# The MLP's last 512 output columns as 384 and 128, with a bank of their own for the 128

## The chip, the cores and the metric

The kernel runs on one core of one Trainium2 chip. The metric is the device time of one execution in microseconds. Of the kernel before three runs were timed; their median is the number to compare with.

## The reference

Two transformer blocks run one after the other on x (256 tokens, width 1024, float32). The change touches only the end of the second block: the squared-ReLU MLP, its residual, and the final norm.

```python
def squared_relu_mlp(h, w_up, w_down):
    a = jax.nn.relu(h @ w_up)
    return (a * a) @ w_down
...
        x = x + squared_relu_mlp(rms_norm(x, g_mlp), w_up, w_down)
    return rms_norm(x, g_final)
```

w_up is 1024 by 4096 and w_down 4096 by 1024. The norm of h multiplies a whole token row by one number r; since relu(a)² scales with r², the kernel leaves r out of the matmuls and multiplies the MLP's output by r² at the end.

## The kernel before

Every product of float32 matrices is made from two parts: `split` turns a piece of weights into a high part `wh` (ACT, rounded to the matmul's format) and a low part `wl` (DVE, the rest), and three matmuls stand for one: high by high, high by low, low by high.

The MLP (`mlp`) works in eight stages of 512 hidden columns. `up` makes a stage's hidden activations `t` (a high and a low tile), `down` multiplies the previous stage's with 512 rows of w_down and adds into four PSUM banks that live through the whole MLP: `acc[c][tt]` for column half c (512 columns) and token tile tt (128 tokens). These banks have the tag "mm"; the hidden activations' sums use the four banks of tag "at".

The last stage is `down_last` (lines 1334 to 1359). It loads both column halves, splits them into four pairs (`parts`), and then runs, for token tile 0 and then 1, and for column half 0 and then 1, a piece of twelve matmuls of 512 columns into `acc[c][tt]`. Behind each piece stand: the update of x on DVE (line 1350, a `scalar_tensor_tensor` that multiplies the bank by r² and adds x), the sum of squares of the 512 columns (`square_sum`, line 651), and the product with the final gain on DVE (line 1352). When both halves of a token tile are done, DVE adds the two sums and epsilon (line 1354), POOL takes the reciprocal root (line 1355), each half is scaled by it (`scaled`, line 646), and SP stores it (line 1359): two stores of 256 KB for each token tile.

The order of instructions on each engine is not the order of writing. All operations are first recorded (`Plan.record`), then `Plan.order` (line 162) runs them through a list of estimated costs (`cost`, line 131) and latencies (line 126): whenever an engine is free, it takes the ready operation with the lowest rank. The rank (line 262) is the index at recording, plus a bias, plus a shift by engine and kind of the output tile:

```python
        prio = [o["i"] + o["bias"] + SHIFT.get((o["engine"], o["kind"]), 0) for o in self.ops]
...
SHIFT = {("tensor", "mm"): 100, ("vector", "wl"): -20}
```

The kind is the tile's tag (line 54). An operation recorded by `either` (line 115) has two forms, one on ACT and one on DVE, and takes the engine that is free first; `square_sum` and `scaled` are such. Matmuls into one bank keep their order. A tag has a fixed number of buffers (4 for `wh`, 4 for `wl`), and a tile's turn comes when an earlier one's last reader is done, so that the four pairs of the last stage are split one by one as the stage before frees them. The resulting order is fixed when the program is built; on the chip each engine goes through its list in order and waits on semaphores.

All instructions carry line 284, the helper that issues them, in the profile, so they are told apart by tile names: `t_mm` and `t_at` are the PSUM banks, `t_p` the scratch that the square sum writes, `t_xg` the product with the gain, `t_rstd` the small tiles of the root.

Of the kernel before, what the change touches and what calls it, by code (L numbers as in the profile page):

```python
# [12 lines left out]
AF = mybir.ActivationFunctionType  # L13
ALU = mybir.AluOpType
AX = mybir.AxisListType

P = 128
# [3 lines left out]
EPS = 1e-6  # L21
# [286 lines left out]
class Kernel:  # L308
# [341 lines left out]

    def square_sum(self, v, ms):

        junk = self.work("p", [P, 512], PB)
        self.nc.either(("scalar", "activation", (junk, v, AF.Square), {"scale": 1.0 / 32.0, "accum_out": ms}),
                       ("vector", "tensor_tensor_reduce", (),
                        {"out": junk, "in0": v, "in1": v, "scale": 1.0 / D, "scalar": 0.0, "op0": ALU.mult,
                         "op1": ALU.add, "accum_out": ms}))
# [635 lines left out]
    def mlp(self, ms):  # L1293
        nc, a = self.nc, self.a
        hT = self.turns("n", [self.x[:, :, :512], self.x[:, :, 512:]], "mlp")
        self.flush("n")
        r = self.rstd(ms)
        r2 = self.work("rstd", [P, 2], 4)
        nc.vector.tensor_tensor(r2, r, r, ALU.mult)
        NS = 8  # L1300
        gb = self.slot([P, D], "gb", F32)
        nc.gpsimd.dma_start(gb, a["g_final_2"].rearrange("(o d) -> o d", o=1).to_broadcast([P, D]))
        xg = [self.slot([P, 2, 512], "xg", F32) for _ in range(2)]

        def square(t, f, n, po):
            r = self.work("tanh", [P, 2, S], 2)[:, :n]
            nc.scalar.activation(r, po, AF.Relu)
            q = self.work("p", [P, 2, S], PB)[:, :n]
            nc.scalar.activation(q, r, AF.Square)
            self.hilo(t[0][:, f:f + n, :], t[1][:, f:f + n, :], q)  # L1310

        def up(s):
            t = self.y_tiles()
            for i in range(2):
                square(t, 2 * i, 2, self.proj_t(a["w_up_2"], 512 * s + 256 * i, hT, tag="at"))
            return t

        def up_first():
            t = self.y_tiles()
            po = [self.psum("at" if f < 2 else "mm")[:, 0] for f in range(4)]  # L1320
            for c in range(2):
                raw = self.load(a["w_up_2"], c * 512, 4, 0, 512)
                for i in range(2):
                    wh, wl = self.split(raw[:, :, 256 * i:256 * i + 256])
                    for f in range(2):
                        fs = slice(f * P, (f + 1) * P)
                        for k in range(4):
                            self.mm3(po[2 * i + f], wh[:, k, fs], wl[:, k, fs], hT(0, 4 * c + k), hT(1, 4 * c + k),
                                     c == 0 and k == 0, c == 1 and k == 3)
            for f in range(4):  # L1330
                square(t, f, 1, po[f].unsqueeze(1))
            return t

        def down_last(s, t):
            parts = [list(self.wide(a["w_down_2"], 512 * s, 4, 512 * c)) for c in range(2)]
            parts = [[(k0, *self.split(v)) for k0, v in half] for half in parts]
            for tt in range(2):
                ts = slice(tt * P, (tt + 1) * P)
                ms = self.work("ms", [P, 2, 2], 4)
                for c in range(2):  # L1340
                    o = acc[c][tt]
                    for k0, wh, wl in parts[c]:
                        for j in range(2):
                            xh, xl = t[0][:, k0 + j, ts], t[1][:, k0 + j, ts]
                            self.nc.tensor.matmul(o, xh, wh[:, j, :], start=False, stop=False)
                            self.nc.tensor.matmul(o, xh, wl[:, j, :], start=False, stop=False)
                            self.nc.tensor.matmul(o, xl, wh[:, j, :], start=False, stop=k0 + j == 3)
                    cs = slice(512 * c, 512 * c + 512)
                    xv = self.x[:, tt, cs]
                    nc.vector.scalar_tensor_tensor(xv, o, r2[:, tt:tt + 1], xv, ALU.mult, ALU.add)  # L1350
                    self.square_sum(xv, ms[:, c, 0:1])
                    nc.vector.tensor_tensor(xg[c][:, tt, :], xv, gb[:, cs], ALU.mult)
                r = self.work("rstd", [P, 2], 4)[:, :1]
                nc.vector.scalar_tensor_tensor(r, ms[:, 0, 0:1], EPS, ms[:, 1, 0:1], ALU.add, ALU.add)
                nc.gpsimd.tensor_tensor(r, r, self.mhalf[:, :1], ALU.pow)
                for c in range(2):
                    v = xg[c][:, tt, :]
                    self.scaled(v, v, r)
                    nc.sync.dma_start(self.out[0, tt * P:(tt + 1) * P, 512 * c:512 * c + 512], v)

        def down(s, t):
            for c in range(2):
                self.proj_n(self.wide(a["w_down_2"], 512 * s, 4, 512 * c), 4, 512, lambda l, k: t[l][:, k, :],
                            banks=acc[c], start=s == 0, stop=False)

        t = up_first()
        acc = [[self.psum("mm", [P, 512]) for _ in range(2)] for _ in range(2)]
        for s in range(NS - 1):
            t2 = up(s + 1)
            down(s, t)  # L1370
            t = t2
        down_last(NS - 1, t)

    def run(self, upto=99):
# [34 lines left out]
PB = 4  # L1409
# [81 lines left out]
```

## Time and profile before

| what | value |
|---|---|
| timed runs | 779.42, 780.11, 781.40 us |
| median | 780.11 us |
| profiled execution | 779.68 us |
| its span, first to last instruction | 777.9 us |
| mean granted clock of TensorE | 0.995 |
| instructions | 11758 |

The profile is of one execution. A line of the timeline has the start, the duration, the engine, the output and input tiles, the shape, and in brackets how long the engine was idle before and what released it. DVE is VectorE, ACT ScalarE, POOL GpSimd, SP SyncE, PE TensorE and PEld its weight loads. The ends of matmuls are modelled, so steps between matmuls are read from start to start. A stretch of busy times gives for each engine the busy time and in brackets the number of instructions.

### The profile page before, as it was taken

What the parts mean: (1) busy time and instruction counts of PE and PEld (TensorE: products, weight loads), DVE (VectorE), ACT (ScalarE), POOL (GpSimd) and SP (SyncE); (2) the same over time, 40 slices, a digit from 0 to 9 for tenths busy, and PEclk for the clock granted to TensorE, in tenths of its full rate; (3) what the DMA queues carried; (4) which work ended last, traced back from release to release, by engine and by line L of the source; (5) the groups of instructions that cost most, each with busy time, mean ns of one, the idle gap of its engine ahead of it and who ended that gap; (6) DMA issues with size and microseconds to landing.
All of it is one profiled execution on the core that took longest, in us unless ns stands there. A gap on an engine that the chain in (4) does not pass through costs nothing.

```text
span 777.9 us, 11758 instructions
## 1 busy us (share of the span) xinstructions
PE 763.1 (98%) x4320; PEld 661.2 (85%) x4320; DVE 620.0 (80%) x1127; ACT 536.8 (69%) x1046; POOL 74.7 (10%) x105
## 2 busy tenths in 40 slices
PE   8989999999999999999999999999999999999996
PEld 7678898888888888888888898799989888888885
DVE  5999998998779889979988889976677655565554
ACT  6697987876679669757787787465556765556552
POOL 0640010000001421132011100100000000000000
PEclk9999999999999999999999999999999999999998
DMA  7796546445558855765348645356535565655631
GB/s 231 244 285 216 162 127 227 138 137 176 184 186 260 237 159 157 210 202 190 115 156 242 191 120 193 105 179 217 181 118 164 177 185 180 215 191 187 210 115 54
DMA packets 109989, 140.48 MB, mean 181 GB/s; under 512 B 3779, under 2 KB 81539, under 8 KB 109932
## 3 DMA queue, kind: packets, MB, share of 16 engines
q1 hardware_dynamic: 104460, 131.64, 52.5%
q0 software_dynamic: 5472, 8.10, 4.7%
q8 instruction: 34, 0.56, 0.3%
q14 instruction: 23, 0.19, 0.1%
HBM read 134.98 MB, written 1.06 MB: 175 GB/s over the span
## 4 chain that ended last, share of the span: by engine, by line
PE 86%; DVE 5%; issue 3%; POOL 2%; ACT 2%; DMA 1%; SPq 0%; POOLq 0%; DVEq 0%; ACTq 0%
PE t_mm L284 64%; PE t_at L284 22%; DVE t_wl L284 2%; DVE t_y L284 1%; POOL t_rrs L284 1%; POOL t_rstd L284 1%; DMA t_xT<-in_x_t_dram 1%; POOL t_ks L284 1%; ACT t_wh L284 0%; DVE t_xs L284 0%; DVE t_p L284 0%; DVE t_x L284 0%; ACT t_p L284 0%; ACT t_xg L284 0%; ACT t_mT L284 0%
## 5 line engine op out<-in xcount | busy, mean ns | idle before, releaser
L284 DVE TENSOR_TENSOR t_wl<-t_raw,t_wh 128x1024 fp32r<-128x1024 f32 (+1 forms) x237 | 288.8, 1219 | 72.6 <-ACT t_wh L284 70.9
L284 ACT ACTIVATE t_wh<-t_raw 128x1024 fp32r<-128x1024 f32 (+1 forms) x237 | 250.4, 1058 | 74.2 <-PE t_mm L284 61.3
L284 PE MATMUL t_mm<-t_mT,t_wh 128*128 128x512 f32 (+1 forms) x512 | 181.6, 394 | 0.4 <-ACT t_wh L284 0.4
L284 PE MATMUL t_mm<-t_mT,t_wl 128*128 128x256 f32 x496 | 131.9, 284 | 0.0
L284 PE MATMUL t_mm<-t_wh,t_yh 128*128 128x512 f32 x288 | 113.5, 394 | 0.0
L284 PE MATMUL t_mm<-t_wh,t_yl 128*128 128x512 f32 x288 | 112.9, 393 | 0.0
L284 PE MATMUL t_mm<-t_wl,t_yh 128*128 128x512 f32 x288 | 112.7, 391 | 0.0
L284 PEld LDWEIGHTS t_mm<-t_mT,t_wh 128*128 128x128 f32 x512 | 93.7, 188 | 14.0 <-ACT t_wh L284 0.8
L284 PEld LDWEIGHTS t_mm<-t_mT,t_wl 128*128 128x128 f32 x496 | 93.4, 189 | 6.5 <-DVE t_wl L284 0.3
L284 PE MATMUL t_at<-t_mT,t_wh 128*128 128x512 f32 (+1 forms) x256 | 85.7, 382 | 0.0
L284 ACT COPY t_sum<-t_mm 128x256 f32<-128x256 f32 x97 | 36.0, 371 | 55.6 <-PE t_mm L284 55.1
L284 PE MATMUL t_mm<-t_wh,t_gh 128*128 128x256 f32 (+2 forms) x256 | 65.9, 339 | 1.5 <-ACT t_wh L284 1.5
L284 PE MATMUL t_at<-t_mT,t_wl 128*128 128x256 f32 x240 | 63.8, 280 | 0.0
L284 PEld LDWEIGHTS t_mm<-t_wh,t_yl 128*128 128x128 f32 x288 | 54.1, 188 | 11.1
L284 PEld LDWEIGHTS t_mm<-t_wl,t_yh 128*128 128x128 f32 x288 | 54.1, 188 | 10.8
L284 PEld LDWEIGHTS t_mm<-t_wh,t_yh 128*128 128x128 f32 x288 | 54.1, 188 | 10.5 <-ACT t_yh L284 0.2
L284 PE MATMUL t_mm<-t_hT,t_wh 128*128 128x512 f32 x168 | 61.8, 400 | 1.0 <-DVE t_sum L284 1.0
L284 ACT ACTIVATE t_p<-t_p,t_st 128x256 f32<-128x256 f32 (+1 forms) x111 | 52.6, 493 | 9.6 <-DVE t_st L284 9.4
L284 POOL TENSOR_TENSOR t_rstd<-t_rstd,t_mhalf 128x2 f32<-128x2 f32 (+1 forms) x12 | 13.3, 1107 | 457.3 <-DVE t_rstd L284 457.3
L284 PEld LDWEIGHTS t_at<-t_mT,t_wh 128*128 128x128 f32 x256 | 45.8, 188 | 6.8
L284 DVE TENSOR_TENSOR t_sum<-t_mm,t_sum 128x256 f32<-128x256 f32 x97 | 40.8, 421 | 13.5 <-ACT t_sum L284 12.7
L284 PEld LDWEIGHTS t_mm<-t_wh,t_gh 128*128 128x128 f32 x256 | 45.1, 194 | 5.9 <-ACT t_wh L284 1.7
(177 smaller groups left out, 1389.1 us busy)
## 6 DMA issues: line engine op xcount, KB each, us to landing
t_raw<-in_w_in_odd_dram SPq DMA_DIRECT2D x20, 1024.0 KB, 5.2
t_raw<-in_w_up_dram SPq DMA_DIRECT2D x16, 1024.0 KB, 5.7
t_raw<-in_w_down_dram SPq DMA_DIRECT2D x16, 1024.0 KB, 5.0
t_raw<-in_w_in_dram SPq DMA_DIRECT2D x12, 1024.0 KB, 5.5
t_raw<-in_w_in_even_dram SPq DMA_DIRECT2D x10, 1024.0 KB, 5.1
t_raw<-in_w_mem_kv_dram SPq DMA_DIRECT2D x8, 1024.0 KB, 5.2
t_raw<-in_w_out_even_dram SPq DMA_DIRECT2D x6, 1024.0 KB, 5.6
t_raw<-in_w_out_odd_dram SPq DMA_DIRECT2D x6, 1024.0 KB, 5.3
```

The costliest lines, as they stand in the source:

```text
L284: f(*[self.real(v) for v in args], **{k: self.real(v) for k, v in kwargs.items()})
```

## The change

In the last stage, token tile 1's second column half is computed as two pieces: columns 0 to 383 into the bank as before, and columns 384 to 511, for this last stage alone, into a bank of their own with the tag "at". The bank `acc[1][1]` keeps the sums of the first seven stages for these 128 columns. After the 384-column piece DVE updates all 512 columns of x from the old bank; a second update then adds the new bank to the last 128. The sum of squares is taken over 384 and over 128 columns apart, a further DVE addition joins the third sum, and the products with the gain for these two cuts are recorded behind the root (`held`). Token tile 0 and all first halves keep pieces of 512.

For both token tiles the scaling is no longer left to `scaled`: DVE scales the first half and the last 128 columns of the second, ACT the other 384. SP stores the first half, and ACT issues the store of the second.

`square_sum` takes as much of its scratch as its input has columns.

```diff
-        junk = self.work("p", [P, 512], PB)
+        junk = self.work("p", [P, 512], PB)[:, :v.shape[-1]]
...
-                ms = self.work("ms", [P, 2, 2], 4)
-                for c in range(2):
-                    o = acc[c][tt]
+                ms = self.work("ms", [P, 2, 2], 4).rearrange("p a b -> p (a b)")
+                held = []
+                cuts = [(0, 0, 512), (1, 0, 512)] if tt == 0 else [(0, 0, 512), (1, 0, 384), (1, 384, 512)]
+                for i, (c, b0, b1) in enumerate(cuts):
+                    bs = slice(b0, b1)
+                    own = b0 > 0
+                    o = self.psum("at", [P, 512])[:, bs] if own else acc[c][tt][:, bs]
                     for k0, wh, wl in parts[c]:
                         for j in range(2):
                             xh, xl = t[0][:, k0 + j, ts], t[1][:, k0 + j, ts]
-                            self.nc.tensor.matmul(o, xh, wh[:, j, :], start=False, stop=False)
-                            self.nc.tensor.matmul(o, xh, wl[:, j, :], start=False, stop=False)
-                            self.nc.tensor.matmul(o, xl, wh[:, j, :], start=False, stop=k0 + j == 3)
-                    cs = slice(512 * c, 512 * c + 512)
+                            self.nc.tensor.matmul(o, xh, wh[:, j, bs], start=own and k0 + j == 0, stop=False)
+                            self.nc.tensor.matmul(o, xh, wl[:, j, bs], start=False, stop=False)
+                            self.nc.tensor.matmul(o, xl, wh[:, j, bs], start=False, stop=k0 + j == 3)
+                    full = slice(512 * c, 512 * c + 512)
+                    cs = slice(512 * c + b0, 512 * c + b1)
+                    if not own:
+                        nc.vector.scalar_tensor_tensor(self.x[:, tt, full], acc[c][tt], r2[:, tt:tt + 1],
+                                                       self.x[:, tt, full], ALU.mult, ALU.add)
                     xv = self.x[:, tt, cs]
-                    nc.vector.scalar_tensor_tensor(xv, o, r2[:, tt:tt + 1], xv, ALU.mult, ALU.add)
-                    self.square_sum(xv, ms[:, c, 0:1])
-                    nc.vector.tensor_tensor(xg[c][:, tt, :], xv, gb[:, cs], ALU.mult)
+                    if own:
+                        nc.vector.scalar_tensor_tensor(xv, o, r2[:, tt:tt + 1], xv, ALU.mult, ALU.add)
+                    self.square_sum(xv, ms[:, i:i + 1])
+                    held.append((xg[c][:, tt, bs], xv, gb[:, cs]))
+                    if b1 - b0 == 512:
+                        nc.vector.tensor_tensor(*held.pop(), ALU.mult)
                 r = self.work("rstd", [P, 2], 4)[:, :1]
-                nc.vector.scalar_tensor_tensor(r, ms[:, 0, 0:1], EPS, ms[:, 1, 0:1], ALU.add, ALU.add)
+                nc.vector.scalar_tensor_tensor(r, ms[:, 0:1], EPS, ms[:, 1:2], ALU.add, ALU.add)
+                if tt == 1:
+                    nc.vector.tensor_tensor(r, r, ms[:, 2:3], ALU.add)
                 nc.gpsimd.tensor_tensor(r, r, self.mhalf[:, :1], ALU.pow)
-                for c in range(2):
-                    v = xg[c][:, tt, :]
-                    self.scaled(v, v, r)
-                    nc.sync.dma_start(self.out[0, tt * P:(tt + 1) * P, 512 * c:512 * c + 512], v)
+                for v in held:
+                    nc.vector.tensor_tensor(*v, ALU.mult)
+                rows = slice(tt * P, (tt + 1) * P)
+                v = [xg[c][:, tt, :] for c in range(2)]
+                nc.vector.tensor_scalar(v[0], v[0], r, None, ALU.mult)
+                nc.sync.dma_start(self.out[0, rows, :512], v[0])
+                nc.scalar.activation(v[1][:, :384], v[1][:, :384], AF.Copy, scale=r)
+                nc.vector.tensor_scalar(v[1][:, 384:], v[1][:, 384:], r, None, ALU.mult)
+                nc.scalar.dma_start(self.out[0, rows, 512:], v[1])
```

## The prediction

> **What bounds the kernel now.** I read the page first (engine shares, chain), then the busy times by stretch over the end of the run, then the timeline there, because the diff edits only the last stage of the MLP.
>
> ```profile
> span 777.9 us, 11758 instructions
> PE 763.1 (98%) x4320; PEld 661.2 (85%) x4320; DVE 620.0 (80%) x1127; ACT 536.8 (69%) x1046; POOL 74.7 (10%) x105
> PE 86%; DVE 5%; issue 3%; POOL 2%; ACT 2%; DMA 1%; SPq 0%; POOLq 0%; DVEq 0%; ACTq 0%
> ```
>
> TensorE is busy for 98% of the span and holds 86% of the chain of waits: a matmul added before its last one lengthens the run, and otherwise only the tail behind the last matmul counts. The next view gives the stretches of the end, columns named in its first line.
>
> ```profile
> core 0: us, PE busy (x) PEld busy (x) DVE busy (x) ACT busy (x) POOL busy (x), PEclk, DMA share, GB/s
> 759.96:762.68 2.72, 2.72 (x14) 2.25 (x13) 1.23 (x1) 1.06 (x1) 0.00 (x0) 1.00 0.00 0
> ...
> 768.12:770.84 2.72, 2.72 (x13) 1.91 (x11) 1.59 (x3) 1.21 (x3) 0.00 (x0) 1.00 0.51 193
> 770.84:773.28 2.44, 0.00 (x1) 0.00 (x0) 1.60 (x3) 0.72 (x2) 0.56 (x1) 1.00 0.00 0
> ...
> 774.63:776.13 1.50, 0.00 (x0) 0.00 (x0) 0.00 (x0) 0.00 (x0) 0.00 (x0) 0.50 0.93 350
> 776.13:777.90 1.77, 0.00 (x0) 0.00 (x0) 0.00 (x0) 0.00 (x0) 0.00 (x0) 0.50 0.00 0
> ```
>
> Each piece of twelve 512-column matmuls (one token tile, one column half) takes 2.72 us on a TensorE without gaps, so 0.227 us a matmul; four such pieces are the last, 759.96 to 770.84. Then comes a tail of 7.06 us: 2.44 to the reciprocal root, the scaling, 1.5 us in which the last 512 KB run at a 0.93 busy DMA, and 1.77 of completion and closing. The timeline of the tail:
>
> ```profile
> 770.45 0.39 PE L284 MATMUL t_mm<-t_wh,t_yl 128*128 128x512 f32 x1
> 770.88 0.75 DVE L284 SCALAR_TENSOR_TENSOR t_x<-t_mm,t_rstd,t_x 128x512 f32<-128x512 f32 x1 [1.13 <-PE t_mm L284]
> 771.66 0.69 DVE L284 TENSOR_TENSOR t_xg<-t_x,t_gb 128x512 f32<-128x512 f32 x1
> 771.72 0.63 ACT L284 ACTIVATE t_p<-t_x 128x512 f32<-128x512 f32 x1 [1.94 <-DVE t_x L284]
> 772.26 0.19 ACT L284 ACTIVATION_READ_ACCUMULATOR t_p<-t_x 128x1 f32 x1
> 772.48 0.16 DVE L284 SCALAR_TENSOR_TENSOR t_rstd<-t_ms 128x1 f32<-128x1 f32 x1
> 772.72 0.56 POOL L284 TENSOR_TENSOR t_rstd<-t_rstd,t_mhalf 128x1 f32<-128x1 f32 x1 [4.88 <-DVE t_rstd L284]
> 773.31 0.72 ACT L284 ACTIVATE t_xg<-t_xg,t_rstd 128x512 f32<-128x512 f32 x1 [0.86 <-POOL t_rstd L284]
> 773.31 0.48 DVE L284 TENSOR_SCALAR t_xg<-t_xg,t_rstd 128x512 f32<-128x512 f32 x1 [0.67 <-POOL t_rstd L284]
> ...
> 773.82 0.81 SPq L284 DMA_DIRECT2D out_dram<-t_xg  x2
> ```
>
> The reader is to see that from the end of the residual update (771.63) to the start of the root (772.72) pass 1.09 us, set by the square sum on ACT; the product with the gain lies beside it.
>
> **Where the planner will put the new matmuls.** The diff's order of writing is not the order of execution. A matmul into tag "mm" has 100 added to its rank (SHIFT, line 1401); the new bank has tag "at", so its twelve 128-column matmuls are ranked some 20 to 35 before even the first piece of tile 0, and go as soon as their weights are split. These rows show when:
>
> ```profile
> 757.28 1.06 ACT L284 ACTIVATE t_wh<-t_raw 128x1024 fp32r<-128x1024 f32 x1 [1.66 <-PE t_mm L284]
> 758.37 1.23 DVE L284 TENSOR_TENSOR t_wl<-t_raw,t_wh 128x1024 fp32r<-128x1024 f32 x1 [1.49 <-ACT t_wh L284]
> ...
> 760.00 1.06 ACT L284 ACTIVATE t_wh<-t_raw 128x1024 fp32r<-128x1024 f32 x1 [1.66 <-PE t_mm L284]
> ...
> 761.09 1.23 DVE L284 TENSOR_TENSOR t_wl<-t_raw,t_wh 128x1024 fp32r<-128x1024 f32 x1 [1.49 <-ACT t_wh L284]
> ```
>
> They are the two weight pairs of the second column half, ready at 759.60 and 762.32. So I expect six narrow matmuls around 758.5 to 760.5 and six around 761.5 to 763.5, and the 384-column piece last on TensorE. (The planner's own durations I use for this order alone.) By that order each narrow matmul stands 0.2 to 0.4 us behind its weights in real time: no stall.
>
> **The cost, part by part.** *TensorE.* Rows for the new widths:
>
> ```profile
> 461.35 0.62 PE L284 MATMUL t_at<-t_ks,t_qs 128*128 128x128 f32 x4
> 461.81 0.39 PE L284 MATMUL t_mm<-t_mT,t_wh 128*128 128x512 f32 x1
> 462.04 0.27 PE L284 MATMUL t_mm<-t_mT,t_wl 128*128 128x256 f32 x1
> ```
> ```profile
> 479.89 0.22 PE L284 MATMUL t_at<-t_ph,t_vp 128*128 128x128 f32 x1
> 479.95 0.28 PE L284 MATMUL t_at<-t_pl,t_vp 128*128 128x128 f32 x1
> 480.06 0.33 PE L284 MATMUL t_mm<-t_mT,t_wl 128*128 128x256 f32 x1
> ```
> ```profile
> 15.64 0.51 PE L284 MATMUL t_mm<-t_wh,t_gh 128*128 128x384 f32 x2
> 15.99 0.33 PE L284 MATMUL t_mm<-t_wl,t_gh 128*128 128x384 f32 x1
> 16.16 0.51 PE L284 MATMUL t_mm<-t_wh,t_gh 128*128 128x384 f32 x2
> ```
>
> Three 384-column matmuls step 16.16 − 15.64 = 0.52, so 0.173 each: twelve save 12 × (0.227 − 0.173) = 0.65. Four 128-column ones step 461.81 − 461.35 = 0.46, so 0.115 each, though 0.057 would be their share by columns; a weight load stands before every matmul (4320 of each). Twelve cost 12 × 0.115 = 1.38. Bounds: 0.06 (479.89 to 479.95) and 0.11 a step (479.95 to 480.06), and 0.173 if they go no faster than the 384s; I take 0.115, the only longer run of this width. TensorE's end: +1.38 − 0.65 = **+0.73** (bounds +0.07 and +1.43).
>
> The Trainium skill ("TensorE: Matmul & The Clock Gate", Back-to-back issue gap) gives about 81 ns for a 128-column pair of weight load and matmul in a stream. By it the estimate for TensorE would be 12 × 0.081 − 0.65 = +0.32 and the whole change +0.93; the row with 0.115 in this number format decides.
>
> *The vector tail.* The full 512-column update of x still stands first and still waits for the whole bank; what follows is now cut in two. Prices:
>
> ```profile
> L284 DVE SCALAR_TENSOR_TENSOR t_p<-t_mm,t_rstd,t_rrs 128x128 f32<-128x128 f32 x2 | 0.7, 349 | 0.4 <-POOL t_rrs L284 0.4
> ...
> L284 DVE TENSOR_TENSOR t_p<-t_p,t_tanh 128x128 f32<-128x128 f32 x2 | 0.6, 283 | 0.0
> ...
> L284 DVE TENSOR_TENSOR t_rstd<-t_ms 128x2 f32<-128x2 f32 x1 | 0.2, 155 | 0.0
> ```
> ```profile
> L284 DVE TENSOR_SCALAR t_p<-t_p,t_st 128x128 f32<-128x128 f32 x5 | 1.4, 286 | 0.2
> ```
> ```profile
> L284 ACT ACTIVATE t_sq<-t_y 128x256 f32<-128x256 f32 x8 | 3.3, 407 | 0.0
> ```
>
> From the end of the full update (0): DVE adds the narrow bank, 0.03 to 0.38. Then the 384-column product: between 0.69 at 512 and 0.28 at 128, so 0.55, 0.41 to 0.96. On ACT the square went from +0.09 to +0.82 (771.72 to 772.45 with its read); 512 to 256 columns saves 0.63 − 0.41 = 0.22, so 384 ends at 0.71, and the new 128-column square, 0.73 − 0.33 = 0.40, at about 1.12. DVE meanwhile does the first sum (0.98 to 1.14) and the 128-column product (1.16 to 1.44), which by rank and readiness the planner starts before the second sum can run, then that sum (1.46 to 1.62). With the same 0.08 to POOL the root starts at 1.70 instead of 1.09: **+0.61**. With the second sum ahead of that product it starts at about 1.43, +0.34; if the split were free, 0. These are the bounds below; above I allow 0.3 more for two extra hand-overs. Three square sums in a row are now on the path where one was.
>
> *Tile 0.* Its scaling adds a 0.29 product to DVE and a store issue to ACT. In 768.12:770.84 DVE is busy 1.59 of 2.72 and ACT 1.21; that stretch shrinks by 0.65 to 2.07, so DVE keeps about 0.2 and ACT, with an issue like SP's 0.4, some 0.4. Hidden, and if the cover is gone the last update starts later by the excess, at most 0.3. Behind ACT's wait for that product only tile 1's first square queues, needed 1 us later.
>
> *Scaling and stores.* After the root DVE does 512 and 128 columns, 0.48 + 0.29, ACT 384: both halves stand by +0.80 against 0.75 now. The first store goes as now; the second can go 0.1 sooner from ACT than behind SP's first issue. But the data run from 774.63 to 776.13 at 0.93 busy without a break between the two stores, so an earlier second one gains nothing: **0**, bounds −0.1 and the price of the second rival. The Trainium skill ("DMA: Bandwidth & Descriptors", Issuing engines are not separate DMA queues) has stores of several engines share the 16 DMA engines and save issue time alone; by it, too, the sum stays.
>
> Sum: 0.73 + 0.61 + 0 = **+1.34 us**. The profiled execution took 779.68 (777.9 span and 1.78 around it): 781.02. It lies 0.43 under the median of 780.11, so as a median I expect 781.45, say **781.4**.
>
> **The rivals.** *The narrow matmuls last, as written* (0.15). The 384 piece then ends at 770.19, its update, square, product and first sum are done by 771.9 behind the narrow matmuls, which end at 771.57; then 0.39 update, 0.51 square, 0.19 sum, 0.08: root at 772.74 instead of 772.72. Time 780.1, no change. For it: the recorded order; against it: the rank without the 100.
>
> *ACT's store lands late* (0.09): the other side. No store from ACT is in this trace; the only queue beside SP's is POOL's:
>
> ```profile
> out_dram<-t_xg SPq DMA_DIRECT2D x4, 256.0 KB, 2.3
> ...
> t_gb<-in_g_final_dram POOLq DMA_DIRECT2D x1, 512.0 KB, 5.4
> ```
>
> If ACT's last store lands like POOL's load, +3.1 on the end: 784.5. It decides from the point where the landing exceeds 2.3 plus the 0.6 that the second store now waits for the data of the first; 1 us more suffices for slower by 0.3%. For it: nothing but that the queue is new. The Trainium skill ("DMA: Bandwidth & Descriptors", SWDGE vs HWDGE vs iDMA) has ACT's DMAs made in hardware like SP's; no run here shows it yet, and it is why I don't go above 0.09.
>
> *A stall from the fixed order* (0.08): if the seventh narrow matmul stood right behind the sixth's weights, TensorE would wait for the second half's low part, from 761.5 to 762.5: +1.0, so 782.4. Against it: the margins above.
>
> *A real gain* (0.04): narrow matmuls last and at 0.06 each; TensorE ends at 770.91, root at 772.08, −0.64: 779.5. Against it: the 0.115.
>
> **How the numbers follow.** Forecast 0.64. A measurement of this kernel can tell about 0.3%, 2.3 us, from no change. The range 779.8 to 783.0 holds the forecast with its bounds (0.07 + 0.34 to 1.43 + 0.9 over the median), the no-change rival and the stall; the late store and the gain lie outside. Faster by over 0.3%: 0.03, since even the last rival reaches only −0.64. Slower by over 0.3% (782.4): the late store, half of the stall, and the forecast's upper corner, 0.13. Same: 0.84.
>
> **What would show it.** Twelve 128-column matmuls before 763.5 and a 384 piece as TensorE's last: order right. The last matmul 0.73 later: step right; a gap of TensorE in the last 11 us: the stall. Update's end to root 1.70. Store data in one stretch of 1.5 us. The prediction is wrong if the end moves by more than 2.3 us, or if the last piece on TensorE is the narrow one.

## The result

| | before | changed |
|---|---|---|
| median of 14 runs each | 780.25 us (779.21 to 783.25) | 782.53 us (780.87 to 785.49) |
| ratio | | 1.0031, 95% interval 1.0019 to 1.0042 |
| profiled execution | 779.68 us, span 777.9 | 782.41 us, span 780.6 |

The changed kernel is slower by 0.3%, just at the size that a measurement can tell. A second timing of it, taken later, gave 1.0020 (1.0007 to 1.0033). The forecast was 781.4 us, in a range of 779.8 to 783.0.

Shares of the engines and of the chain of waits, changed kernel:

```profile
span 780.6 us, 11790 instructions
...
PE 763.9 (98%) x4332; PEld 662.5 (85%) x4332; DVE 620.3 (79%) x1132; ACT 536.1 (69%) x1048; POOL 74.4 (10%) x105
...
PE 87%; DVE 5%; issue 3%; POOL 2%; ACT 1%; DMA 1%; SPq 0%; POOLq 0%; DVEq 0%; ACTq 0%
```

Twelve matmuls more, PE busy for 0.8 us more, and nothing else to be seen: these shares hide what changed in the last 20 us. The timeline of TensorE's matmuls (start, duration, operation, tiles, shape):

```profile
759.05 0.22 PE L284 MATMUL t_at<-t_wh,t_yh 128*128 128x128 f32 x1
759.11 0.45 PE L284 MATMUL t_mm<-t_wl,t_yh 128*128 128x512 f32 x1
759.39 0.39 PE L284 MATMUL t_mm<-t_wh,t_yl 128*128 128x512 f32 x1
...
760.38 0.27 PE L284 MATMUL t_at<-t_wh,t_yl 128*128 128x128 f32 x1
760.49 0.28 PE L284 MATMUL t_at<-t_wh,t_yh 128*128 128x128 f32 x1
...
763.70 0.27 PE L284 MATMUL t_at<-t_wh,t_yl 128*128 128x128 f32 x1
...
764.10 0.40 PE L284 MATMUL t_mm<-t_wh,t_yl 128*128 128x512 f32 x1
...
769.77 0.33 PE L284 MATMUL t_mm<-t_wh,t_yh 128*128 128x384 f32 x1
...
771.71 0.34 PE L284 MATMUL t_mm<-t_wh,t_yl 128*128 128x384 f32 x1
```

The twelve narrow matmuls (into `t_at`) lie between 759.05 and 763.70, the 384-column piece stands last. A narrow one steps 0.11 within a bunch. Where a single one stands between 512-column matmuls, the next starts after 0.06, but that next one takes 0.28 to the one behind it, and not 0.23: the price is 0.11 there too. Over the whole stretch from 759.05 to 764.10, 5.05 us, stand the twelve and sixteen 512-column matmuls; without the sixteen at 0.227 each, 0.118 is left for a narrow one, because the 512-column steps among them are up to 0.01 longer. The timeline of all engines, cut to the second-last weight conversion (ACT's `t_wh`) and the tail:

```profile
757.66 1.06 ACT L284 ACTIVATE t_wh<-t_raw 128x1024 fp32r<-128x1024 f32 x1 [1.66 <-PE t_mm L284]
...
770.29 0.74 DVE L284 SCALAR_TENSOR_TENSOR t_x<-t_mm,t_rstd,t_x 128x512 f32<-128x512 f32 x1
...
770.74 2.78 ACTq L284 DMA_DIRECT2D out_dram<-t_xg  x1
...
772.09 0.75 DVE L284 SCALAR_TENSOR_TENSOR t_x<-t_mm,t_rstd,t_x 128x512 f32<-128x512 f32 x1 [0.33 <-PE t_mm L284]
...
773.56 0.63 ACT L284 ACTIVATE t_p<-t_x 128x512 f32<-128x512 f32 x1 [3.26 <-DVE t_x L284]
...
774.19 0.51 ACT L284 ACTIVATE t_p<-t_x 128x384 f32<-128x384 f32 x1
...
774.70 0.29 ACT L284 ACTIVATE t_p<-t_x 128x128 f32<-128x128 f32 x1
...
775.12 0.16 DVE L284 TENSOR_TENSOR t_rstd<-t_rstd,t_ms 128x1 f32<-128x1 f32 x1
...
775.35 0.55 POOL L284 TENSOR_TENSOR t_rstd<-t_rstd,t_mhalf 128x1 f32<-128x1 f32 x1 [5.70 <-DVE t_rstd L284]
```

ACT's row of 2.78 us is the term that the forecast's sum lacked: the issue of tile 0's second store. Tile 1's first square could run from 771.03, when its update of 770.29 ended, but ACT was issuing until 773.52. All three squares of tile 1 then ran in one row behind it, and the root started 2.52 us after the end of the last update (772.83 to 775.35), where it was 1.09 in the kernel before. The bracket of the 773.56 row blames DVE's `t_x`; that was ready long before.

To compare executions I count from the start of the second-last weight conversion on ACT (757.28 before, 757.66 here; an expectation below calls the same one the third-last), because it starts anywhere from 757.28 to 761.50 in the profiles here, and up to it all engines run the same instructions in the same order with and without the change. The span grows so:

| stretch, us | before | changed | difference |
|---|---|---|---|
| span start to that conversion | 757.28 | 757.66 | +0.38 |
| conversion to the start of the last full update | 13.60 | 14.42 | +0.82 |
| end of that update to root | 1.09 | 2.52 | +1.43 |
| root to end | 5.19 | 5.20 | 0 |

The update itself takes 0.75 in both. The sum, 2.63, is the difference of the spans, 780.55 − 777.91 = 2.64.

### The profile page after: what moved, and what is told of

Read it like the earlier page. It is cut to its first block, busy times and chain, and to the rows that moved or that the text cites. A ratio compares the mean times of both kernels' runs of the same rounds, so it can differ in the third digit from the quotient of the medians.

```text
span 780.6 us, 11790 instructions
## 1 busy us (share of the span) xinstructions
PE 763.9 (98%) x4332; PEld 662.5 (85%) x4332; DVE 620.3 (79%) x1132; ACT 536.1 (69%) x1048; POOL 74.4 (10%) x105
## 4 chain that ended last, share of the span: by engine, by line
PE 87%; DVE 5%; issue 3%; POOL 2%; ACT 1%; DMA 1%; SPq 0%; POOLq 0%; DVEq 0%; ACTq 0%
PE t_mm L284 65%; PE t_at L284 22%; DVE t_wl L284 1%; DVE t_y L284 1%; POOL t_rrs L284 1%; POOL t_rstd L284 1%; DMA t_raw<-in_w_in_even_dram 1%; POOL t_ks L284 1%; ACT t_wh L284 0%; DVE t_xs L284 0%; DVE t_p L284 0%; DVE t_x L284 0%; DVE t_xg L284 0%; ACT t_mT L284 0%; DVE t_hT L284 0%
## 5 line engine op out<-in xcount | busy, mean ns | idle before, releaser
L284 PE MATMUL t_mm<-t_wh,t_yh 128*128 128x512 f32 (+1 forms) x288 | 113.4, 394 | 0.0
L284 PE MATMUL t_mm<-t_wl,t_yh 128*128 128x512 f32 (+1 forms) x288 | 112.7, 391 | 0.0
L284 PE MATMUL t_mm<-t_wh,t_yl 128*128 128x512 f32 (+1 forms) x288 | 112.7, 392 | 0.0
```

The source lines that it names most:

```text
L284: f(*[self.real(v) for v in args], **{k: self.real(v) for k, v in kwargs.items()})
```

## The experiments

All are edits of the changed kernel, or that kernel again, and each profiled execution is read by the same stretches, in us. "Ratio" is to the kernel before, timed beside it; kernels without a ratio were only profiled.

| kernel | ratio (95% interval) | conversion to start of last full update | end of that update to root | conversion to root | ACT's store issues |
|---|---|---|---|---|---|
| before | | 13.60 | 1.09 | 15.44 | |
| changed | 1.0031 (1.0019 to 1.0042) | 14.42 | 2.52 | 17.69 | 2.78, 0.34 |
| all stores on SP | 0.9991 (0.9978 to 1.0004) | 14.42 | 1.27 | 16.44 | |
| sharing alone | 1.0007 (0.9993 to 1.0020) | 13.60 | 1.03 | 15.38 | 0.38, 0.34 |
| 128 last | 1.0001 (0.9988 to 1.0014) | 12.99 | 1.65 | 15.39 | |
| small ACT transfer at the start | 1.0009 (0.9996 to 1.0022) | 14.42 | 1.27 | 16.44 | 0.35, 0.34 |
| ACT for the last store only | 1.0011 (1.0000 to 1.0022) | 14.42 | 1.27 | 16.45 | 0.38 |
| cut alone | 1.0013 (1.0001 to 1.0025) | 14.43 | 1.27 | 16.45 | |
| small ACT transfer at the MLP | none | 14.42 | 1.27 | 16.44 | 0.35, 0.34 |
| 256 and 256, own bank last | 0.9992 (0.9980 to 1.0003) | 12.38 | 1.99 | 15.12 | |
| changed, second profile | 1.0020 (1.0007 to 1.0033) | 14.42 | 2.52 | 17.69 | 2.78, 0.34 |
| changed, third profile | none | 14.42 | 1.27 | 16.44 | 0.37, 0.34 |
| small ACT transfer at the start, again | 0.9997 (0.9985 to 1.0009) | 14.42 | 1.27 | 16.44 | 0.35, 0.34 |
| changed, fourth profile | none | 14.42 | 2.52 | 17.69 | 2.78, 0.34 |

**All stores on SP.** Does the long issue alone make the 1.43?

```diff
-                nc.scalar.dma_start(self.out[0, rows, 512:], v[1])
+                nc.sync.dma_start(self.out[0, rows, 512:], v[1])
```

> The changed kernel with both second-half stores issued by SP again; cut and scaling stay. First theory (ACT's first store issue of 2.78 us holds up tile 1's first square sum): ACT has no long issue, from the end of the 512-column update to the root it takes 1.70 us instead of 2.51, TensorE's end stays 0.8 late, and the end comes 0.8 us before the changed kernel's, some +1.5 on the kernel before. Rival (three square sums in a row are simply dearer than the 0.61 I gave them): the 2.51 stay, and so does the time.

Its timeline behind the last update:

```profile
771.76 0.75 DVE L284 SCALAR_TENSOR_TENSOR t_x<-t_mm,t_rstd,t_x 128x512 f32<-128x512 f32 x1 [0.32 <-PE t_mm L284]
772.54 0.35 DVE L284 SCALAR_TENSOR_TENSOR t_x<-t_at,t_rstd,t_x 128x128 f32<-128x128 f32 x1
772.60 0.52 ACT L284 ACTIVATE t_p<-t_x 128x384 f32<-128x384 f32 x1 [1.14 <-DVE t_x L284]
772.81 0.55 DVE L284 TENSOR_TENSOR t_xg<-t_x,t_gb 128x384 f32<-128x384 f32 x1
773.03 0.19 ACT L284 ACTIVATION_READ_ACCUMULATOR t_p<-t_x 128x1 f32 x1
773.12 0.29 ACT L284 ACTIVATE t_p<-t_x 128x128 f32<-128x128 f32 x1
773.28 0.15 DVE L284 SCALAR_TENSOR_TENSOR t_rstd<-t_ms 128x1 f32<-128x1 f32 x1
...
773.35 0.29 DVE L284 TENSOR_TENSOR t_xg<-t_x,t_gb 128x128 f32<-128x128 f32 x1
773.55 0.15 DVE L284 TENSOR_TENSOR t_rstd<-t_rstd,t_ms 128x1 f32<-128x1 f32 x1
773.78 0.56 POOL L284 TENSOR_TENSOR t_rstd<-t_rstd,t_mhalf 128x1 f32<-128x1 f32 x1 [4.45 <-DVE t_rstd L284]
```

From 772.51 to 773.78 pass 1.27 us: the split of the tail costs 0.18, where the expectation's 1.70 had it at 0.61, and the other 1.25 of the 1.43 was the long issue. TensorE's term is as in the changed kernel, 14.42.

**Sharing alone.** The scaling and the stores as in the change, but no cut.

```diff
-                cuts = [(0, 0, 512), (1, 0, 512)] if tt == 0 else [(0, 0, 512), (1, 0, 384), (1, 384, 512)]
+                cuts = [(0, 0, 512), (1, 0, 512)]
```

> The second part of the change alone: all pieces 512 wide as before, but DVE and ACT share the scaling and ACT issues the second stores. First theory: ACT's store of tile 0 is issued for some 2.8 us, from about 768.9 to 771.7 of the span, tile 1's two square sums run one behind the other after it, the root starts 0.66 us late and the end comes 0.7 later than before. Rival: the issue is harmless and the time is that of before, since the root waits for the last update anyway.

```profile
775.21 0.56 POOL L284 TENSOR_TENSOR t_rstd<-t_rstd,t_mhalf 128x1 f32<-128x1 f32 x1 [4.82 <-DVE t_rstd L284]
775.79 0.62 ACT L284 ACTIVATE t_xg<-t_xg,t_rstd 128x384 f32<-128x384 f32 x1 [0.86 <-POOL t_rstd L284]
775.79 0.68 DVE L284 TENSOR_SCALAR t_xg<-t_xg,t_rstd 128x512 f32<-128x512 f32 x2 [0.67 <-POOL t_rstd L284]
776.31 0.36 SPq L284 DMA_DIRECT2D out_dram<-t_xg  x1
776.57 0.34 ACTq L284 DMA_DIRECT2D out_dram<-t_xg  x1
```

SP and ACT issue their stores at once, 0.26 us apart, and from the root to the end it is still 5.19 us. The sharing gains nothing and costs nothing in this execution. ACT's issue in tile 0 took 0.38 here, so ACT doesn't always need 2.8; what a long one would cost without the cut, the +0.66 of the expectation, no run shows.

**Small ACT transfer ahead.** If a first transfer of ACT costs something once, a tiny one early in the run takes it off the tail. 512 bytes into a tile that nobody reads, issued by ACT at the start of the run; a second kernel issues it where the MLP begins, at 586.67 us.

```diff
         for i in seq:
+            if i == self.mark:
+                self.nc.scalar.dma_start(self.first, self.rows)
```

> The changed kernel plus one DMA of 512 bytes issued by ACT at the start of the run, into a tile that nobody reads; all other instructions in the same order. If the long issue belongs to the first DMA that ACT issues in a run: the small DMA takes some 2.8 us at the start, tile 0's store by ACT takes 0.34 as tile 1's did, update to root is 1.70, and the end is 0.8 us earlier than the changed kernel's, unless the start is delayed. If it belongs to the place (SP's store issued just before, or the load at the end): tile 0's store still takes 2.8.

> The changed kernel plus one DMA of 512 bytes by ACT at the start of the MLP. If ACT's code for DMAs, once used, stays ready for the some 150 us to the end: tile 0's store takes 0.34 and update to root is 1.70, and the small DMA itself takes 2.8 at its place. If the store still takes 2.8, the cost is of the place or comes back after other work of ACT.

Timeline of the first of the two, ACT's queue:

```profile
770.30 0.35 ACTq L286 DMA_DIRECT2D out_dram<-t_xg  x1
...
775.31 0.34 ACTq L286 DMA_DIRECT2D out_dram<-t_xg  x1
```

Both stores are issued at 0.35 and 0.34, but the tiny transfer itself took no more than 0.41 (0.38 in the second kernel). So it isn't a price that every first transfer of ACT pays: here nobody paid it. That theory falls; that a first transfer is long in some executions only, these two profiles don't exclude.

**ACT for the last store only.** Tile 0's stores both on SP, so that ACT issues a single transfer, its last instruction.

```diff
-                nc.scalar.dma_start(self.out[0, rows, 512:], v[1])
+                (nc.sync if tt == 0 else nc.scalar).dma_start(self.out[0, rows, 512:], v[1])
```

> The changed kernel with tile 0's two stores on SP and ACT issuing only tile 1's second store. If the long issue belongs to ACT's first DMA: it now stands at the very end, behind the scaling; update to root is 1.70, the last store is issued for 2.8 us and its data run 2.4 later, so the end comes some 1.6 us later than the changed kernel's (0.8 gained, 2.4 lost), +3.9 on before. If it belongs to tile 0's place: the last store takes 0.34 and the end is that of the kernel with all stores on SP, +1.5 on before.

Issue 0.38, root at 16.45 behind the conversion, root to end 5.19: ACT's first transfer is short here too.

**Cut alone.** The cut as the planner orders it, with the scaling and the four SP stores of before.

```diff
-                v = [xg[c][:, tt, :] for c in range(2)]
...
+                for c in range(2):
+                    v = xg[c][:, tt, :]
+                    self.scaled(v, v, r)
+                    nc.sync.dma_start(self.out[0, rows, 512 * c:512 * c + 512], v)
```

> The first part of the change alone: the cut with the planner's own order (narrow matmuls early), scaling and stores as before. Theory: TensorE's end 0.7 to 0.85 late, update to root 1.70 instead of 1.09, end some +1.4 on before; the difference to the narrow matmuls last is what the order costs, 1.3. Rival: the cut costs nothing and the whole loss is ACT's store: time of before.

```profile
758.78 1.06 ACT L284 ACTIVATE t_wh<-t_raw 128x1024 fp32r<-128x1024 f32 x1 [1.66 <-PE t_mm L284]
...
773.21 0.75 DVE L284 SCALAR_TENSOR_TENSOR t_x<-t_mm,t_rstd,t_x 128x512 f32<-128x512 f32 x1 [0.52 <-PE t_mm L284]
...
775.23 0.55 POOL L284 TENSOR_TENSOR t_rstd<-t_rstd,t_mhalf 128x1 f32<-128x1 f32 x1 [4.46 <-DVE t_rstd L284]
```

Root at 16.45 (758.78 to 775.23) against 15.44: the cut costs 1.01 us, all that the change costs when no issue is long.

**128 last.** Cut alone, and the narrow matmuls held back to the place where they are written.

```diff
+                    nc.bias = 200 if own else 0
                     for k0, wh, wl in parts[c]:
```

> Cut only, scaling and stores as before, and the narrow matmuls ranked behind the 384-column piece (200 added to their rank). Theory by the recorded rivals: TensorE still ends 0.7 to 0.8 late, but the 384-column update, square and product lie under the narrow matmuls, so the root starts 0.0 to 0.1 later than before and the time is that of before. If instead the order makes no difference: root 1.4 later, +1.4.

```profile
770.42 0.75 DVE L284 SCALAR_TENSOR_TENSOR t_x<-t_mm,t_rstd,t_x 128x512 f32<-128x512 f32 x1 [0.52 <-PE t_mm L284]
...
771.39 0.28 PE L284 MATMUL t_at<-t_wh,t_yl 128*128 128x128 f32 x1
771.71 0.35 DVE L284 SCALAR_TENSOR_TENSOR t_x<-t_at,t_rstd,t_x 128x128 f32<-128x128 f32 x1
...
772.15 0.31 ACT L284 ACTIVATE t_p<-t_x 128x128 f32<-128x128 f32 x1 [0.27 <-DVE t_rstd L284]
...
772.82 0.56 POOL L284 TENSOR_TENSOR t_rstd<-t_rstd,t_mhalf 128x1 f32<-128x1 f32 x1 [4.83 <-DVE t_rstd L284]
```

The full update now runs beside the narrow matmuls, and from the last matmul's start to the root pass 1.43 us (771.39 to 772.82), where before it is 2.27 (770.45 to 772.72). These 0.84 are what the cut can win; the later start of TensorE's last matmul, 13.96 against 13.17 behind the conversion, takes 0.79 of them back.

**256 and 256, own bank last.** The same with a wider second piece.

```diff
-                cuts = [(0, 0, 512), (1, 0, 512)] if tt == 0 else [(0, 0, 512), (1, 0, 384), (1, 384, 512)]
+                cuts = [(0, 0, 512), (1, 0, 512)] if tt == 0 else [(0, 0, 512), (1, 0, 256), (1, 256, 512)]
```

> Tile 1's second half as two pieces of 256, the second in its own bank and last on TensorE, scaling and stores as before. By the rows: 24 matmuls of 256 columns at 0.117 take 0.09 more than 12 of 512; behind the last one stand a 256-column update (0.48), square (0.5), sum and hand-overs, 1.39 to the root instead of 1.88. Theory: root and end 0.4 us earlier than before, too little for the timed runs to tell (ratio 0.9995). Rival (hand-overs and the third square eat it): root not earlier than before.

```profile
769.46 0.28 PE L284 MATMUL t_at<-t_wh,t_yh 128*128 128x256 f32 x1
...
770.78 0.28 PE L284 MATMUL t_at<-t_wh,t_yl 128*128 128x256 f32 x1
771.10 0.48 DVE L284 SCALAR_TENSOR_TENSOR t_x<-t_at,t_rstd,t_x 128x256 f32<-128x256 f32 x1 [0.17 <-PE t_at L284]
...
771.68 0.42 ACT L284 ACTIVATE t_p<-t_x 128x256 f32<-128x256 f32 x1 [0.60 <-DVE t_rstd L284]
...
772.46 0.56 POOL L284 TENSOR_TENSOR t_rstd<-t_rstd,t_mhalf 128x1 f32<-128x1 f32 x1 [4.56 <-DVE t_rstd L284]
```

A 256-column matmul steps 0.12 (769.46 to 770.78 in eleven), hardly more than a 128-column one for twice the columns. TensorE's last matmul starts 0.26 later than before (13.43 against 13.17), the tail from there to the root is 1.68, so 0.59 shorter, and the root starts 0.32 earlier than before. By the profile it is the best of the kernels; halves in the planner's own order were not run. Its ratio, 0.9992 (0.9980 to 1.0003), lies below that of the change, but doesn't tell it from the kernel before.

**The changed kernel again.** Is the long issue an accident of one execution?

> The changed kernel again, unaltered, profiled afresh and timed in 5 rounds. Theory A (ACT's 2.78 us store issue in tile 0 was an accident of one execution: the 8 KB instruction load that fell into it comes near 759 us in other executions): the first ACT store is issued in 0.34 to 0.41 us, from the end of the last update to the root 1.27 us, the last root 16.44 us behind the third-last weight conversion's start, the 8 KB load near 758 to 761 us, and the ratio to the kernel before nearer to 1.001 (structural cost 1.00 us of 780, 1.0013) than to 1.0031. Theory B (this program, as it lies in memory, always fetches there): issue 2.6 to 2.9 us, update to root 2.5 us, root 17.7 us behind that start, ratio 1.002 to 1.004.

> The changed kernel once more, one look. Theory A: as in most executions, ACT's first store issued in 0.34 to 0.41 us and update to root 1.27 us. Theory B: 2.6 to 2.9 us and 2.5 us again. A mixture over the looks at this kernel (some 2.8, some 0.4) would mean that where the 8 KB load falls changes from execution to execution.

> The warm-start kernel again (the changed kernel with one 512-byte transfer by ACT at the start of the run), profiled afresh and timed in 5 rounds; the looks at the changed kernel so far had ACT's first store issue at 2.78, 2.78 and 0.37 us. Theory A (where the 8 KB load falls varies by execution in any of these programs): the 2.78 us issue can turn up here as well, and the ratio is that of the changed kernel, 1.002 to 1.003. Theory B (one more ACT instruction ahead moves the place at which the code is fetched): issue 0.34 to 0.41 us as the first time, 8 KB load near 759 us, update to root 1.27 us, ratio near 1.001.

> The changed kernel a fourth time, one look. Both theories allow either issue here: 2.78 us with the 8 KB load inside it, update to root 2.52 us; or 0.34 to 0.41 us with the load near 759 to 763 us and update to root 1.27 us. What neither allows is a long issue without the load inside it, or the load inside a short one.

It came in three of four profiles, at 2.78 each time, so it is no accident, and in the third it did not, so it isn't fixed by the program either. The third:

```profile
774.29 0.37 ACTq L284 DMA_DIRECT2D out_dram<-t_xg  x1
774.89 0.63 ACT L284 ACTIVATE t_p<-t_x 128x512 f32<-128x512 f32 x1 [0.76 <-DVE t_x L284]
...
777.94 0.55 POOL L284 TENSOR_TENSOR t_rstd<-t_rstd,t_mhalf 128x1 f32<-128x1 f32 x1 [4.46 <-DVE t_rstd L284]
```

With a short issue the first square runs as soon as its update ends, and the root follows the last update by 1.27. What goes with the long issue is seen in the DMA view. In the changed kernel's first profile, between 757.5 and 764.0:

```profile
DMA packets 0, 0.00 MB, mean 0 GB/s; under 512 B 0, under 2 KB 0, under 8 KB 0
```

The same profile during the issue, 770.74 to 773.53, by queue and kind (packets, MB, share of the 16 DMA engines):

```profile
q1 hardware_dynamic: 144, 0.26, 25.5%
q14 instruction: 1, 0.01, 0.7%
```

And in its third profile, between 761.0 and 764.5:

```profile
q14 instruction: 1, 0.01, 0.8%
```

Queue 14, of kind "instruction", moves one packet of 8 KB near the end of the run. In the third profile it starts at 762.67, 1.18 us behind the conversion; so it does, at 1.14 to 1.50, in every profile of every other kernel, before included. In the three profiles with a long issue it is missing there and starts 1.3 us into the issue, at 772.02 in the first. As the expectation of the fourth profile asked, there was no long issue without the load inside it, and no load inside a short one. Which of the two brings about the other is not shown by this.

The kernel with the small transfer at the start, profiled again, had 0.35 again, and a ratio of 0.9997. With one ACT instruction more ahead, three profiles of two programs showed the load early, against one of four without it. That may speak for the place in the instruction stream. But sharing alone and ACT for the last store only, whose ACT instructions are those of the changed kernel up to tile 0's store, with none ahead, showed the load early as well, so it isn't settled.

Loads of this queue move elsewhere too. One that lies in the kernel before at 307.0 us lies at 316.5 in the changed kernel's first profile and at 317.8 in cut alone, which has no store on ACT. Between 314 and 318 the steps between ACT's rows in the changed kernel are those of the kernel before to within 0.02 us, so a late load of this queue doesn't always cost time, and it needs no store on ACT to be late. For which engine that load is, no view says.

## Why the prediction was right, and where not

*Order of the narrow matmuls: right.* Expected at about 758.5 to 760.5 and 761.5 to 763.5, seen at 759.05 to 760.8 and 761.81 to 763.8, and no gap on TensorE. The rank without the 100 did what the listing said.

*TensorE +0.73: right in kind, +0.82 measured* (14.42 against 13.60), the same in every kernel with the cut in the planner's order. The 384-column matmuls step 0.176 (769.77 to 771.71 in eleven) against 0.173, and the narrow ones cost 0.118 each over their whole stretch against 0.115; the two differences, twelve times each, make about 0.07 of the 0.09. The Trainium skill ("TensorE: Matmul & The Clock Gate", Back-to-back issue gap) has about 81 ns for a pair of weight load and 128-column matmul. The traces here differ: 0.11 us in a bunch, and the measurement decides.

*The vector tail +0.61: mis-sized.* Without the long issue it is +0.18 (1.27 against 1.09). The step that failed is the adding of durations end to end. In the stores-on-SP timeline, rows of one engine overlap: the 384-column square lasts 0.52 from 772.60, but its read starts at 773.03 and the next square at 773.12; the second sum starts at 773.55, while the 128-column product before it runs to 773.64. On DVE, which the forecast had as the path to the root, the steps from start to start are 0.27, 0.47, 0.07 and 0.20 (772.54 to 773.55), 1.01 in all, where the forecast's were 0.38, 0.57, 0.18 and 0.30, 1.43 in all: that is the 0.43. Such steps would have shown it, and the prediction's own rows had one on ACT: 771.72 + 0.63 is 772.35, and the read stood at 772.26. So the lower corner that was worked out from rows, +0.34, was too high as well; only the bound of 0 for a free split lay below.

*Tile 0 hidden: the step that failed for this kernel.* It was costed as "an issue like SP's 0.4", with a loss of at most 0.3 if the cover is gone. With an issue of 0.35 to 0.38 it is hidden indeed: the stretch to the last update is 14.42 with and without ACT's store. But the price of ACT's issue had no row, and it was bounded by the nearest one on another engine alone. The text bounded the loss by DVE's next update, the wrong victim, though it named what queues behind ACT (tile 1's first square, needed 1 us later). An issue of 2.78 uses up the 1 us and delays the root by 1.25.

*Scaling and stores 0: right.* Root to end is 5.19 or 5.20 in all kernels.

*The sum.* +1.34 was forecast for the profiled execution. Measured without the long issue: 0.82 + 0.18 = 1.00; with it 2.25, and 0.38 more upstream. Besides +0.09 on TensorE, two errors of opposite sign, −0.43 on the tail and +1.25 on the issue, left the total within the range: that the number fits is luck in part. The prediction named a move of the end by more than 2.3 us as a sign of being wrong; the medians moved by 2.28 and the profiled spans by 2.64, so that sign was met in the profile and just missed in the medians. Another sign was 1.70 us from the update's end to the root, where 2.52 and 1.27 were found. If the issue is long in three executions of four, as in the four profiles, the mean is 1.00 + 0.75 × 1.25 = 1.94 us, a ratio of 1.0025: between the two that were timed.

*The rivals.* The narrow matmuls last were priced rightly, root +0.02 expected and −0.05 found, but the planner didn't do it. No stall arose. ACT's store doesn't land late; the DMA issues of the changed kernel's third profile:

```profile
out_dram<-t_xg SPq DMA_DIRECT2D x2, 256.0 KB, 2.1
out_dram<-t_xg ACTq DMA_DIRECT2D x2, 256.0 KB, 2.5
```

In the first profile the last one took 2.5 as well; tile 0's, with the long issue, took 4.5.

This agrees with the rule of the Trainium skill cited for that rival: ACT's transfers behave like SP's. The rival had looked at the landing of the last store; the price turned up at the issue of the first.

## What to carry to other kernels

Cutting the last piece paid here only with the small part ending last: find out where the scheduler puts it, because in this change the part with a bank of its own went to the front and the tail kept all its work and an extra sum. Choose the cut by the step per matmul and not by the columns: 128 columns cost 0.11 us and 256 cost 0.12, so with the own bank last halves won 0.32 where 384 and 128 won 0.05. In the planner's order 384 and 128 lost 1.0. Cost a tail from start to start of rows, and give a store issue on a compute engine a bound of its own, named with the instruction that stands behind it.

## What was not expected of the hardware

ACT's issue of a 256 KB store took 0.34 to 0.38 us in all but three cases, and 2.78 in those, each time with an 8 KB load of kind "instruction" (0.3 us long) inside it. All three were the first transfer that ACT issued in the run, while six other first ones took 0.37 to 0.41. That ACT was waiting for its own next instructions is the reading that suggests itself; it isn't shown, since no view says for whom the load is, and why the load came 13 us later in these executions than in the others stays open, as does how often it does so in runs without a profile.

Times of kernels whose tails agree to 0.01 us differ by 1.7 us, more than the 1.0 that the cut costs: all stores on SP 0.9991, cut alone 1.0013, with intervals that overlap only from 1.0001 to 1.0004. The conversion that I count from started at 757.34 in one profile and 758.78 in the other, and what lies around the span was 1.77 us in the median of the one and 2.14 of the other, so 0.37 of the 1.7 us is outside the span; the rest stays open. For steps of 1 us in 780 the stretches of the profile decide, and the ratio only bounds them.
